# A matmul unit takes its last chunk at its very end, and background work of a decoder layer begins later

## The chip, the cores and the metric

The kernel runs on one core of a Trainium2 chip. The metric is the device time of one execution in microseconds; the median over several runs is compared. The engines of the core run their own instruction streams and meet at semaphores: TensorE (PE: matmuls), VectorE (DVE), ScalarE (ACT), GpSimd (POOL), and SyncE (SP), which issues the DMAs. The order of instructions on each engine is fixed when the program is built.

## The reference, cut to what matters

One layer of a decoder, in float32, for 512 prompt tokens and 64 sample tokens (576 in all) of width 1024:

```python
def swiglu(x, w_gate, w_up, w_down):
    return (jax.nn.silu(x @ w_gate) * (x @ w_up)) @ w_down

def decoder_layer(x, conv4_buf, lru_h0, conv31_buf, mem_k, mem_v, p):
    x = x + FFN_RES * rmsnorm(swiglu(rmsnorm(x, p['g_ff1_pre']), p['ff1_w_gate'], p['ff1_w_up'], p['ff1_w_down']), p['g_ff1_post'])
    mix, new_conv4, new_h, new_conv31 = token_mixer(rmsnorm(x, p['g_mix_pre']), conv4_buf, lru_h0, conv31_buf, p)
    x = x + rmsnorm(mix, p['g_mix_post'])
    x = x + rmsnorm(memory_attention(rmsnorm(x, p['g_mem_pre']), mem_k, mem_v, p['w_q'], p['w_o']), p['g_mem_post'])
    x = x + FFN_RES * rmsnorm(swiglu(rmsnorm(x, p['g_ff2_pre']), p['ff2_w_gate'], p['ff2_w_up'], p['ff2_w_down']), p['g_ff2_post'])
    return x, new_conv4, new_h, new_conv31
```

The hidden width of the two feed-forward blocks is 2816, which is 22 chunks of 128. The token mixer has a causal convolution over 31 positions, for which the sample tokens need 30 old rows of state each.

## The kernel before

**Products.** Every float32 operand is split in two parts, a first (h) and a second (l), and a matmul becomes three products: weight h by input h, weight h by input l ("highs"), and weight l by input h ("lows"). The 576 tokens are two halves of 288 columns. A *unit* is one output tile of 128 rows; for each half `mm` issues its products into one bank of PSUM: for 8 input chunks 16 highs and then 8 lows, 24 in all (21 for 7 chunks). `flow.until(... in xs.ready)` in `mm` lets the planner run until an input chunk has been planned; on the chip the product then waits for the semaphore of the engine that makes the chunk.

**Feed-forward.** `f1` and `f2` run in three groups of 8, 7 and 7 hidden chunks. In a group, each chunk has a gate unit and an up unit (`f1g`), and the result goes DVE, ACT, DVE, ACT, DVE: `f1s` (normalised gate product out of PSUM), silu on ACT, `f1u` (up product), `f1s<-f1s,f1u`, then `f1h_h` on ACT (first part) and `f1h_l` on DVE (second part). Behind the group come 8 down units (`f1d`) that take those chunks as their input, so the first down unit's last chunk is the one made last. The down sums are added up in `f1o` by DVE.

**Weights.** Each unit's weights come by DMA (`wraw`), ACT makes the first part (`wspl<-wraw`), POOL the second in four pieces of 256 columns (DVE at times). For 33 of the later units the second part is made ahead of time by `make_lows`: DMA in (`kraw`), a copy on ACT and a subtraction on DVE (both `khi`), and a DMA out to memory (`lows`), from which the unit loads it. Two such ways run side by side. They pause from two units before to the end of an edge between up and down units (`HOLD`).

**Old rows.** `old_rows` computes the part of the 31-tap convolution that depends on the old state only: for each of four pairs of chunks a DMA each (`st`, two buffers), one ACT instruction each, and 29 small DVE instructions each (`old<-st,par,old`), 232 on DVE and 8 on ACT in all. They don't pause at edges. The buffers of a pair are loaded again when DVE has read the pair before for the last time.

**What sets the order.** `Flow` is a planner that runs while the program is built. It keeps a made-up clock which the products push forward, and generators that yield until a time on that clock; the order in which they come up is the order of the instructions on every engine. `make_lows` starts at `KEPTAT` (its second way `KEPTGAP` later) and rests `KEPTGAP` after each piece, `old_rows` starts at `OLDROWS` and yields `OGAP` after each step. So what changes a planned time anywhere can move instructions later in the program too.

Of the kernel before, what the change touches and what calls it, by code (L numbers as in the profile page):

```python
# [65 lines left out]
X1 = 8  # L66
XSQ = 0.3
XSL = 2
OLDROWS = 80
OGAP = 1  # L70
KEPTAT = 25
KEPTGAP = 5
HOLD = 2
MEMORY = 150
MSL = 1
# [217 lines left out]
def trunk(ctx: ExitStack, tc: tile.TileContext, I, O):  # L293
# [6 lines left out]
    def dma(out, in_, eng=nc.sync):  # L300
        eng.dma_start(out=out, in_=in_)
        n = 1
        for _, c in out.ap:
            n *= c
        t = max(flow.now, flow.busy.get("d", 0.0)) + n * 4 / 300e3
        flow.busy["d"] = t
        flow.write(out, t + 2.0)

    def product(out, lhsT, rhs, start=True, stop=True):
        nc.tensor.matmul(out, lhsT, rhs, start=start, stop=stop)  # L310
        n = width(rhs)
        cost = 0.001 + max(n, 192) * 0.000457 if rhs.dtype == F32R else max(0.11, n * 0.00084)
        flow.product(cost, (lhsT, rhs), out)
# [16 lines left out]
    def bank(name):  # L330
        return psp.tile([P, 512], F32, tag="ps", name=name)
# [97 lines left out]
    def highs(ps, w, k, xs, half):  # L429

        hi, lo = xs.at(k, half)
        flow.settle(hi, lo)
        product(ps[:, :H], w[:, 0, k, :], hi, start=k == 0, stop=False)
        product(ps[:, :H], w[:, 0, k, :], lo, start=False, stop=False)

    def lows(ps, unit, xs, half):
        w, nk = unit
        for k in range(nk):
            product(ps[:, :H], w[:, 1, k, :], xs.at(k, half)[0], start=False, stop=k == nk - 1)
            flow.run()  # L440

    def mm(unit, xs, half, name):

        w, nk = unit
        ps = bank(name)
        for k in range(nk):
            flow.until(lambda: (k, half) in xs.ready)
            highs(ps, w, k, xs, half)
            flow.run()
        lows(ps, unit, xs, half)  # L450
        return ps

    def units_of(n, lead, xs, name, window=0):


        order = stream(n, lead, 0)
        if window:
            for at in range(0, n, window):
                us = [next_unit(j == 0) for j in range(window)]
                for half in range(2):  # L460
                    for j, u in enumerate(us):
                        if half and j:
                            ahead(state["used"] - window + j)
                        yield at + j, half, mm(u, xs, half, f"{name}_{at + j}_{half}")
            return
        for i, halves in order:
            u = next_unit()
            for half in halves:
                yield i, half, mm(u, xs, half, f"{name}_{i}_{half}")
# [102 lines left out]
    def fresh(name, n=KC):  # L572
        o = Operand(n)
        for c in range(n):
            o.hi[c], o.lo[c] = ring(f"{name}h{c}", F32R), ring(f"{name}l{c}", F32R)
        return o
# [227 lines left out]
    def project(o, xs, first, tail, name, lag=0, end=None):  # L804
# [38 lines left out]
        for m, halves in stream(n, 0, lag):  # L843
            u = next_unit()
            for half in halves:
                flow.spawn(evac(m, half, mm(u, xs, half, f"{name}_{m}_{half}")))
# [59 lines left out]
    def old_rows():  # L906

        for c0 in range(0, KC, 2):
            both = range(c0, c0 + 2)
            st = {}  # L910
            for c in both:
                st[c] = memp.tile([P, NB * GL], F32, tag="st", name=f"st{c}", bufs=2)
                dma(out=st[c], in_=I["conf_state"][c])
            yield wait(*st.values())
            for c in both:
                act.activation(out=tok(old[:, c, :]), in_=st[c].rearrange("p (b t) -> p b t", t=GL)[:, :, 0:NT],
                               func=AF.Identity, scale=cw[:, 0, c:c + 1], bias=V["conf_conv_b"][:, c:c + 1])
            for k in range(1, GS):
                yield OGAP
                n = min(NT, GS - k)  # L920
                for c in both:
                    o = tok(old[:, c, :])[:, :, :n]
                    vec.scalar_tensor_tensor(out=o, in0=st[c].rearrange("p (b t) -> p b t", t=GL)[:, :, k:k + n],
                                             scalar=cw[:, k, c:c + 1], in1=o, op0=ALU.mult, op1=ALU.add)

    def memory():
        raw = [memp.tile([P, 2 * NM], F32, tag=f"raw{q}", name=f"mraw{q}") for q in range(KC // 2)]
        for q in range(KC // 2):
            dma(out=raw[q].rearrange("p (c t) -> p c t", c=2),
                in_=I["mem"][2 * q:2 * q + 2].rearrange("c p t -> p c t"))  # L930
        x = [raw[c // 2][:, c % 2 * NM:(c % 2 + 1) * NM] for c in range(KC)]
        sqs = Squares(accs[2], KC, "mem")
        for c in range(KC):
            yield wait(x[c]) + 1
            sqs.add(x[c], NM)
        yield from sqs.whole()
        rbs = []
        yield from bcast_rsqrt(accs[2], "mem", rbs, 0, NM)
        yield wait(rbs[0])
        for c in range(KC):  # L940
            vec.scalar_tensor_tensor(out=x[c], in0=x[c], scalar=V["g_mem_kv"][:, c:c + 1], in1=rbs[0][:, :NM],
                                     op0=ALU.mult, op1=ALU.mult)
        for c in range(KC):
            t = ring(f"mT{c}", F32R)
            yield wait(x[c]) + 1
            split(t[:, 0:NM], t[:, NM:2 * NM], x[c], vec, lambda t=t: mT.append(t))

    def make_lows(way):

        for n, (src, nk, ncol) in enumerate(makes):  # L950
            if n % 2 != way:
                continue
            while any(e - HOLD <= state["used"] <= e for e in edges):
                yield 0.5
            cols = slice(0, nk * ncol)
            raw = memp.tile([P, 1024], F32, tag=f"kraw{way}", name=f"kraw{n}")
            hi = memp.tile([P, 1024], F32R, tag=f"khi{way}", name=f"khi{n}")
            dma(out=raw[:, cols].rearrange("p (k m) -> p k m", k=nk), in_=src)
            yield wait(raw)
            act.activation(out=hi[:, cols], in_=raw[:, cols], func=AF.Copy)  # L960
            yield wait(hi)
            vec.tensor_tensor(out=hi[:, cols], in0=raw[:, cols], in1=f32(hi[:, cols]), op=ALU.subtract)
            yield wait(hi) + 0.5
            dma(out=lows_[n, :, cols], in_=f32(hi[:, cols]))
            yield KEPTGAP

    for way in range(2):
        flow.spawn(make_lows(way), KEPTAT + way * KEPTGAP)
    flow.spawn(memory(), MEMORY)
    flow.spawn(old_rows(), OLDROWS)  # L970
    mixin = ffn("f1", F1LEAD, xg, ghalf[:, 0, :], V["g_mix_pre"], lambda: fresh("mn"), place=0, rbx=rbx)
# [13 lines left out]
    for m in range(KC):  # L985
        w, _ = next_unit()
        ps = bank(f"mk{m}")
# [318 lines left out]
    for m, half, ps in first4:  # L1306
        lows(ps, us[m], yl, half)
# [439 lines left out]
```

## Time and profile before

| | |
|---|---|
| median of 3 runs | 1474.09 us (1473.46 to 1474.64) |
| the profiled execution | 1476.8 us |
| its span in the trace | 1475.0 us |
| TensorE busy | 1422.6 us (96%) |
| VectorE busy | 879.8 us (60%) |
| GpSimd busy | 817.4 us (55%) |
| ScalarE busy | 723.5 us (49%) |
| mean granted clock of TensorE | 0.982 |

TensorE is busy for nearly the whole span, so the time is its work, its idle time, and what its clock adds when it is granted at half. The stages by time: `f1` to about 402 us and its last down units behind that, the mixer's input products (`z`), its output products (`wol`, `woc`), the queries, attention (about 910 to 1010), and `f2` to the end.

### The profile page before, as it was taken

The numbers are of one execution on the slowest core, as the hardware profiler recorded it, in microseconds if no ns is written. First come the engines' busy times: TensorE is split into PE (matmuls) and PEld (weight loads), VectorE is DVE, ScalarE is ACT, GpSimd is POOL, SyncE is SP. The second block draws the span as 40 slices with busy tenths as digits, with TensorE's granted clock in tenths as the row PEclk, the third lists the DMA queues.
The fourth block names the chain that finished last, engine by engine and source line by source line (L and its number), as shares of the span: only waits on it lengthen the run. The fifth ranks groups of instructions, "written<-read, shape, count | busy, mean of one in ns | idle before, by whom it ended". The sixth has DMA issues, their size and how long they took to land.

```text
span 1475.0 us, 27481 instructions
## 1 busy us (share of the span) xinstructions
PE 1422.6 (96%) x10550; PEld 1408.8 (96%) x10550; DVE 879.8 (60%) x1737; ACT 723.5 (49%) x1269; POOL 817.4 (55%) x1005
## 2 busy tenths in 40 slices
PE   8999999999999999999899999978999999999997
PEld 8999999999999999998699999878999999999997
DVE  7877887423356699999986776863633012312335
ACT  7544534322355568657847577764532222212233
POOL 7854445544356777676745566742464444444433
PEclk9999999999999999999999999998999999999998
DMA  6775766632388433223436787873642222222244
GB/s 234 224 264 182 250 216 228 211 89 85 116 291 306 131 106 93 92 92 123 160 117 223 259 297 268 278 274 126 232 151 86 75 84 85 76 88 85 80 137 140
DMA packets 89299, 245.34 MB, mean 166 GB/s; under 512 B 11984, under 2 KB 26576, under 8 KB 89168
## 3 DMA queue, kind: packets, MB, share of 16 engines
q1 hardware_dynamic: 84560, 235.66, 48.2%
q10 hardware_dynamic: 4608, 7.93, 1.5%
q8 instruction: 83, 1.36, 0.4%
q14 instruction: 48, 0.39, 0.1%
HBM read 215.76 MB, written 27.80 MB: 165 GB/s over the span
## 4 chain that ended last, share of the span: by engine, by line
PE 69%; DVE 19%; ACT 4%; POOL 3%; issue 3%; DMA 2%; SPq 0%; DVEq 0%; ACTq 0%; POOLq 0%
PE f2g L310 18%; PE f1g L310 13%; PE f2d L310 10%; PE f1d L310 9%; DVE cv L258 5%; PE z L310 3%; PE wol L310 3%; PE wo L310 3%; POOL wspl L258 2%; PE q L310 2%; PE woc L310 2%; DVE u L258 2%; PE mk L310 2%; DVE acc L258 1%; DVE cc L258 1%
## 5 line engine op out<-in xcount | busy, mean ns | idle before, releaser
L258 POOL TENSOR_TENSOR wspl<-wraw,wspl 128x256 fp32r<-128x256 f32 x840 | 654.1, 811 | 521.9 <-ACT wspl L258 518.0
L258 ACT ACTIVATE wspl<-wraw 128x1024 fp32r<-128x1024 f32 (+1 forms) x267 | 276.7, 1037 | 273.2 <-PE f2g L310 113.0
L310 PE MATMUL f1g<-xgh,wspl 128*128 128x288 f32 x1408 | 284.9, 297 | 0.0
L310 PE MATMUL f2g<-fnh,wspl 128*128 128x288 f32 x1408 | 281.3, 295 | 0.0
L310 PEld LDWEIGHTS f1g<-xgh,wspl 128*128 128x128 f32 x1408 | 228.2, 190 | 0.4 <-ACT xgh L258 0.2
L310 PEld LDWEIGHTS f2g<-fnh,wspl 128*128 128x128 f32 x1408 | 226.8, 188 | 0.0
L310 PE MATMUL z<-mnh,wspl 128*128 128x288 f32 x1024 | 206.0, 297 | 3.8 <-DVE gl L258 3.8
L310 PE MATMUL f1g<-xgl,wspl 128*128 128x288 f32 x704 | 192.0, 298 | 1.8 <-DVE xgl L258 1.8
L310 PE MATMUL f2g<-fnl,wspl 128*128 128x288 f32 x704 | 189.5, 295 | 0.0
L310 PEld LDWEIGHTS z<-mnh,wspl 128*128 128x128 f32 x1024 | 165.7, 190 | 4.2 <-issue 4.2
L310 PE MATMUL f1d<-f1h_h,wspl 128*128 128x288 f32 x704 | 143.9, 299 | 2.4 <-ACT f1h_h L258 2.4
L310 PE MATMUL f2d<-f2h_h,wspl 128*128 128x288 f32 x704 | 140.8, 295 | 0.0
L310 PE MATMUL z<-mnl,wspl 128*128 128x288 f32 x512 | 138.7, 297 | 0.0
L310 PEld LDWEIGHTS f1g<-xgl,wspl 128*128 128x128 f32 x704 | 133.7, 190 | 3.0 <-DVE xgl L258 2.7
L258 DVE SCALAR_TENSOR_TENSOR cv<-gl,par,cv 128x512 f32<-128x512 f32 x194 | 133.8, 745 | 0.0
L310 PEld LDWEIGHTS f2g<-fnl,wspl 128*128 128x128 f32 x704 | 132.5, 188 | 0.0
L310 PEld LDWEIGHTS f1d<-f1h_h,wspl 128*128 128x128 f32 x704 | 115.1, 191 | 2.6 <-ACT f1h_h L258 2.6
L310 PEld LDWEIGHTS f2d<-f2h_h,wspl 128*128 128x128 f32 x704 | 113.1, 188 | 0.0
L310 PE MATMUL f1d<-f1h_l,wspl 128*128 128x288 f32 x352 | 96.5, 299 | 0.7 <-DVE f1h_l L258 0.7
L258 DVE TENSOR_TENSOR f2u<-rbt,f2g 128x288 f32<-128x288 f32 x44 | 20.0, 454 | 129.1 <-PE f2g L310 129.1
L310 PEld LDWEIGHTS z<-mnl,wspl 128*128 128x128 f32 x512 | 96.8, 189 | 0.0
L310 PE MATMUL f2d<-f2h_l,wspl 128*128 128x288 f32 x352 | 94.8, 295 | 0.0
(324 smaller groups left out, 2661.2 us busy)
## 6 DMA issues: line engine op xcount, KB each, us to landing
wraw<-in_ff_w_gate SPq DMA_DIRECT2D x51, 512.0 KB, 3.7
wraw<-in_ff_w_up SPq DMA_DIRECT2D x50, 512.0 KB, 3.6
wspl<-lows SPq DMA_DIRECT2D x42, 512.0 KB, 4.2
wraw<-in_ff_w_down SPq DMA_DIRECT2D x46, 448.0 KB, 4.0
wraw<-in_w_in SPq DMA_DIRECT2D x32, 512.0 KB, 3.9
lows<-khi SPq DMA_DIRECT2D x26, 512.0 KB, 3.6
wraw<-in_w_out SPq DMA_DIRECT2D x24, 512.0 KB, 4.2
wraw<-in_ff_w_down SPq DMA_DIRECT2D x16, 512.0 KB, 3.6
```

Of the source, the lines that this page charges most:

```text
L258: return fn(*a, **k)
L310: nc.tensor.matmul(out, lhsT, rhs, start=start, stop=stop)
```

## The change

In `mm`, the last chunk's highs come behind the lows of all the other chunks, and its low last: for 8 chunks 14 highs, 7 lows, then 2 highs and 1 low. The last chunk is thus first used by product 22 rather than product 15 (for 7 chunks product 19 rather than 13). One other user of `highs` and `lows`, the first four units of `wol`, is as before. Three constants of the planner change: old rows start at 140 rather than 80, second parts made ahead at 130 rather than 25, and they rest 3 rather than 5.

```diff
-OLDROWS = 80
+OLDROWS = 140
 OGAP = 1
-KEPTAT = 25
-KEPTGAP = 5
+KEPTAT = 130
+KEPTGAP = 3
...
-    def lows(ps, unit, xs, half):
+    def lows(ps, unit, xs, half, ks=None):
         w, nk = unit
-        for k in range(nk):
+        for k in range(nk) if ks is None else ks:
             product(ps[:, :H], w[:, 1, k, :], xs.at(k, half)[0], start=False, stop=k == nk - 1)
             flow.run()
...
         for k in range(nk):
+            if k == nk - 1:
+
+                lows(ps, unit, xs, half, range(nk - 1))
             flow.until(lambda: (k, half) in xs.ready)
             highs(ps, w, k, xs, half)
             flow.run()
-        lows(ps, unit, xs, half)
+        lows(ps, unit, xs, half, (nk - 1,))
         return ps
```

The count of instructions on PE, ACT and POOL work is the same but for a few pieces that go to DVE instead of POOL. In the rows below a name carries the group, the chunk and the half (`f1s1_6_0`: group 1 of 0 to 2, chunk 6, half 0), and a running number of the tile.

DVE's instructions at the end of group 0, before, from the last chunk's first evacuation to its second part:

```order
L258 TENSOR_TENSOR f1s0_7_0_1536<-rbt_155,f1g0_14_0_1416 128x288
L258 TENSOR_TENSOR f1u0_7_0_1537<-rbt_155,f1g0_15_0_1497 128x288
L258 SCALAR_TENSOR_TENSOR old_161<-st0_1104,par_103,old_161 128x8x3
L258 SCALAR_TENSOR_TENSOR old_161<-st1_1106,par_103,old_161 128x8x3
L258 TENSOR_TENSOR f1s0_7_0_1536<-f1s0_7_0_1536,f1u0_7_0_1537 128x288
L258 SCALAR_TENSOR_TENSOR old_161<-st0_1104,par_103,old_161 128x8x2
L258 SCALAR_TENSOR_TENSOR old_161<-st1_1106,par_103,old_161 128x8x2
L258 SCALAR_TENSOR_TENSOR old_161<-st0_1104,par_103,old_161 128x8
L258 SCALAR_TENSOR_TENSOR old_161<-st1_1106,par_103,old_161 128x8
L258 TENSOR_TENSOR f1s0_7_1_1581<-rbt_155,f1g0_14_1_1461 128x288
L258 TENSOR_TENSOR f1u0_7_1_1582<-rbt_155,f1g0_15_1_1533 128x288
L258 TENSOR_TENSOR f1h0_l7_185<-f1s0_7_0_1536,f1h0_h7_184 128x288
```

The same place in the changed kernel:

```order
L258 TENSOR_TENSOR f1h0_l6_183<-f1s0_6_1_1316,f1h0_h6_182 128x288
L258 TENSOR_TENSOR f1s0_7_0_1412<-rbt_155,f1g0_14_0_1313 128x288
L258 TENSOR_TENSOR f1u0_7_0_1413<-rbt_155,f1g0_15_0_1379 128x288
L258 TENSOR_TENSOR f1s0_7_0_1412<-f1s0_7_0_1412,f1u0_7_0_1413 128x288
L258 TENSOR_TENSOR f1h0_l7_185<-f1s0_7_0_1412,f1h0_h7_184 128x288
```

No old row and no `khi` stands in group 0 any more; twelve old rows had also stood between `f1h0_l6` and `f1s0_7_0` before. The first `khi` now comes with the first down unit, and the first old rows a little behind it.

DVE at the end of group 1, before:

```order
L258 TENSOR_TENSOR f1h1_l5_2256<-f1s1_5_1_3235,f1h1_h5_2255 128x288
L258 TENSOR_TENSOR f1s1_6_0_3332<-rbt_155,f1g1_12_0_3232 128x288
L258 TENSOR_TENSOR f1u1_6_0_3333<-rbt_155,f1g1_13_0_3299 128x288
L258 TENSOR_TENSOR f1s1_6_0_3332<-f1s1_6_0_3332,f1u1_6_0_3333 128x288
L258 TENSOR_TENSOR f1h1_l6_2258<-f1s1_6_0_3332,f1h1_h6_2257 128x288
```

And in the changed kernel, where ten old rows of the fourth pair stand between `f1h1_l5` and the first row shown:

```order
L258 TENSOR_TENSOR f1s1_6_0_3218<-rbt_155,f1g1_12_0_3101 128x288
L258 TENSOR_TENSOR f1u1_6_0_3219<-rbt_155,f1g1_13_0_3179 128x288
L258 SCALAR_TENSOR_TENSOR old_161<-st6_3113,par_103,old_161 128x64
L258 SCALAR_TENSOR_TENSOR old_161<-st7_3115,par_103,old_161 128x64
L258 TENSOR_TENSOR f1s1_6_0_3218<-f1s1_6_0_3218,f1u1_6_0_3219 128x288
L258 SCALAR_TENSOR_TENSOR old_161<-st6_3113,par_103,old_161 128x64
L258 SCALAR_TENSOR_TENSOR old_161<-st7_3115,par_103,old_161 128x64
L258 SCALAR_TENSOR_TENSOR old_161<-st6_3113,par_103,old_161 128x64
L258 SCALAR_TENSOR_TENSOR old_161<-st7_3115,par_103,old_161 128x64
L258 TENSOR_TENSOR f1s1_6_1_3259<-rbt_155,f1g1_12_1_3145 128x288
L258 TENSOR_TENSOR f1u1_6_1_3260<-rbt_155,f1g1_13_1_3215 128x288
L258 TENSOR_TENSOR f1h1_l6_2069<-f1s1_6_0_3218,f1h1_h6_2068 128x288
```

Sixteen old rows have moved ahead of the second part on which the first down unit of group 1 waits. On ACT the fourth pair's start now stands right ahead of the same chunk's silu:

```order
L258 ACTIVATE f1s1_5_1_3104<-f1s1_5_1_3104 128x288
L258 ACTIVATE f1h1_h5_2066<-f1s1_5_1_3104 128x288
L258 ACTIVATE old_161<-st6_3113,par_103 128x64
L258 ACTIVATE old_161<-st7_3115,par_103 128x64
L258 ACTIVATE wspl46_3178<-wraw46_3002 128x896
L258 ACTIVATE f1s1_6_0_3218<-f1s1_6_0_3218 128x288
L258 ACTIVATE f1h1_h6_2068<-f1s1_6_0_3218 128x288
```

The two old instructions are new at this place; the rest of these rows stood there before in the same order. Some pieces of the mixer and of attention change places by a few instructions as well.

## Rows read from the trace of the kernel before

**Rows 1.** The page: part 1, and two lines of part 2 (40 slices).
```profile
PE 1422.6 (96%) x10550; PEld 1408.8 (96%) x10550; DVE 879.8 (60%) x1737; ACT 723.5 (49%) x1269; POOL 817.4 (55%) x1005
...
PEclk9999999999999999999999999998999999999998
```

**Rows 2.** Waits of TensorE by what released it: total, times, longest (us).
```profile
PE sot L310 <- ACT so L258: 6.9, 2, 6.4
PE wol L310 <- DVE yll L258: 4.1, 1, 4.1
...
PE f1d L310 <- ACT f1h_h L258: 2.4, 1, 2.4
...
PE spt L364 <- DVE ssum L258: 2.0, 2, 1.2
...
PE f1d L310 <- DVE f1h_l L258: 0.7, 1, 0.7
```

**Rows 3.** Timeline of TensorE at the first down unit: start, length, idle before.
```profile
120.65 0.29 PE L310 MATMUL f1d<-f1h_h,wspl 128*128 128x288 f32 x1
...
125.05 0.46 PE L310 MATMUL f1d<-f1h_h,wspl 128*128 128x288 f32 x1 [2.38 <-ACT f1h_h L258]
126.25 0.61 PE L310 MATMUL f1d<-f1h_l,wspl 128*128 128x288 f32 x1 [0.73 <-DVE f1h_l L258]
126.65 2.36 PE L310 MATMUL f1d<-f1h_h,wspl 128*128 128x288 f32 x9
```

**Rows 4.** Stretches: TensorE busy (products), granted clock, DMA share; last one `f2d` alone.
```profile
120.65:178.80 58.15, 55.04 (x396) 0.94 0.70 238
125.24:132.07 6.83, 6.10 (x25) 0.50 0.80 249
...
1142.37:1193.38 51.01, 51.01 (x384) 1.00 0.27 82
```

**Rows 5.** Timeline of VectorE at the first group's end.
```profile
114.98 1.75 DVE L258 TENSOR_TENSOR khi<-kraw,khi 128x1024 fp32r<-128x1024 f32 x1
116.66 2.84 DVE L258 SCALAR_TENSOR_TENSOR old<-st,par,old 128x64 f32<-128x64 f32 x4
119.43 1.01 DVE L258 TENSOR_TENSOR f1h_l<-f1s,f1h_h 128x288 fp32r<-128x288 f32 x1
120.37 2.75 DVE L258 SCALAR_TENSOR_TENSOR old<-st,par,old 128x64 f32<-128x64 f32 x12
123.04 0.44 DVE L258 TENSOR_TENSOR f1s<-rbt,f1g 128x288 f32<-128x288 f32 x1
...
125.75 0.44 DVE L258 TENSOR_TENSOR f1h_l<-f1s,f1h_h 128x288 fp32r<-128x288 f32 x1
```

**Rows 6.** Timeline of VectorE at the second group's end.
```profile
264.86 0.46 DVE L258 TENSOR_TENSOR f1u<-rbt,f1g 128x288 f32<-128x288 f32 x1 [1.19 <-PE f1g L310]
...
266.56 0.46 DVE L258 TENSOR_TENSOR f1h_l<-f1s,f1h_h 128x288 fp32r<-128x288 f32 x1 [0.51 <-ACT f1h_h L258]
```

**Rows 7.** Old rows: ns min/median/max; then one pair's start on ScalarE and VectorE.
```profile
L258 DVE SCALAR_TENSOR_TENSOR old<-st,par,old x232: 220/274/785, 93.4 to 240.8; 128x64 f32<-128x64 f32 x88, 128x56 f32<-128x56 f32 x4, 128x48 f32<-128x48 f32 x4, 128x40 f32<-128x40 f32 x4
...
205.71 0.44 ACT L258 ACTIVATE old<-st,par 128x64 f32<-128x64 f32 x1 [4.31 <-DMA st<-in_conf_state]
...
202.79 1.40 DVE L258 SCALAR_TENSOR_TENSOR old<-st,par,old 128x8 f32<-128x8 f32 x2
...
207.85 0.87 DVE L258 SCALAR_TENSOR_TENSOR old<-st,par,old 128x64 f32<-128x64 f32 x4
```

**Rows 8.** Two other waits of TensorE, and the clock of the stretches with them.
```profile
38.54 0.83 PE L310 MATMUL ssx<-ones,acc 128*128 128x1 f32 x6 [2.27 <-DVE acc L258]
...
703.18 0.40 PE L310 MATMUL lg<-xch,gwh 128*128 128x288 f32 x1 [2.34 <-DVE xc L258]
...
39.90:43.30 3.40, 3.40 (x16) 0.50 0.61 244
702.00:706.60 4.60, 3.42 (x16) 1.00 0.08 15
```

## The prediction, made before the changed kernel was run

> **What bounds the kernel now.** I read the page first, then TensorE's waits, then the stretches in which its clock is low, and only then the engine that made it wait. The page shows TensorE busy for 1422.6 of 1475.0 us [rows 1]; the reader sees that no other engine is near that, and that the granted clock is full in nearly every slice. So the work of TensorE is a floor that this change does not touch (the same products, in another order). What can move is its 52 us of idle time and the stretches at half clock that follow some waits. The list of waits [rows 2] has one entry that this change aims at: the first down unit of `f1` waits 2.38 us for `f1h_h` and 0.73 us for `f1h_l`. The others in that list lie in the mixer and in attention.
>
> The place itself: the first down unit starts at 120.65, has done its 14 highs of seven chunks, and stands until 125.05 and again until 126.25 [rows 3]. From 125.24 to 132.07 the clock granted is 0.50, which is the 1.2 GHz level, and 25 products take 6.10 us there [rows 4]. Elsewhere a product takes 51.01 / 384 = 0.133 us, from the down units of `f2`, which wait for nothing [rows 4]; 25 of them would be 3.32 us. So the half clock costs 2.78 us, the waits 3.11 us, and the place 5.9 us. As a check: `f1`'s eight units of this kind take 58.15 us and `f2`'s 51.01 [rows 4], 7.1 us more, of which the remaining 1.25 us belong to the 12 other products that stand among them.
>
> Why it waited: the up unit's half 0 of the last chunk ended 24 products before 120.65, at 117.46, but DVE took it out of PSUM only at 123.04 and gave the second part at 126.19, 8.7 us after the product. DVE had no gap since 114.98: one `khi` of 1.75 us, four old rows of 0.71 each, a second part of 1.01, twelve old rows of 0.23 each [rows 5]. Where DVE has neither old rows nor `khi` in front of it, at the end of group 1, the way from the released evacuation (264.86) to the second part (267.02) is 2.2 us [rows 6]. DVE, late with background work, bounds this place.
>
> **The change, part by part.**
>
> *Edge of group 0.* All old rows and all `khi` leave group 0. The last chunk then takes about 2.2 us, ready near 119.7, ahead of the down unit's start; its half 1, whose up unit ends at 120.65, is ready by about 123 and is needed only after 24 + 21 products, 6.0 us. Both waits go, and the half clock that came with them: -5.9 us. The new order of products alone would give 7 products, 0.93 us, of the 3.1.
>
> *Where the work goes.* The 33 second parts and 232 old rows still have to be done before the units that use them. DVE, ACT and the DMA queue have room in the down units of group 0, where DVE has no chunks to make. That part I cost at nothing: TensorE waits there for weights alone, none of which waits is in the list [rows 2]. If the cover were gone, the price would be a wait for `wspl`; before, the same DMA load beside the first down units (share 0.70 to 0.80, [rows 4]) caused none.
>
> *Edge of group 1.* Before, it cost nothing: the last chunk was made in 2.2 us [rows 6]. Now the fourth pair of old rows stands there: on DVE ten rows ahead of the last chunk's first evacuation, six more ahead of its second part; on ACT the pair's start right ahead of the chunk's silu. Queued behind them are `f1s`, `f1u`, `f1h_h` and `f1h_l` of that chunk, and for those the first down unit of group 1 waits. The time allowed, from the end of up half 0: its half 1, 24 products, then 18 products before the last chunk is used, and one more before its second part, 43 x 0.133 = 5.7 us. The old order would allow 0.8 us less.
>
> What the chunk takes now is not shown, so I bound it. From below 2.2 us, if DVE has caught up by then [rows 6]: no wait. From above 8.7 us, the last chunk of group 0 with sixteen old rows and a `khi` close in front [rows 5]: a wait of 3.0 us. In between: 2.2 us, plus sixteen old rows at 0.23, the price of the twelve in one run, 3.7 us, plus about half of a pair's start. A pair's start holds both engines: the old pair's last row ended at 204.19, the next pair's first began at 207.85, and ACT stood 4.31 us for the transfer [rows 7]. It takes 3.7 us, and I count 2 of them, since it begins ahead of the up unit's half. That is 7.9 us, a wait of 2.2 us. I take it rather than the upper bound since no `khi` of 1.75 us stands in that run.
>
> Whether the clock then falls is at its limit: a wait of 2.27 us at 38.54 was followed by a stretch at 0.50, one of 2.34 us at 703.18 by none [rows 8]. I take it that it does not fall at 2.2; if it falls, the price is that of the first edge, 2.8 us.
>
> Here a rule speaks against the change. The rows show one old row taking from 0.22 to 0.79 us, median 0.27 [rows 7], and the four slow ones at 116.66 stand beside the fast ones at 120.37 [rows 5]. The Trainium skill (GPSIMD Engine Reference, 1. Specifications) says that GpSimd shares its SBUF interfaces with VectorE and collides with its instructions that have two SBUF inputs; an old row has two, and the trace's two levels agree. By that rule the rows moved to group 1 run at the price that GpSimd's splits happen to leave them, which is the third rival below.
>
> *The rest.* In the mixer and in attention some pieces change places by a few instructions. The waits there are 6.9 us for `so`, 4.1 for `yll`, 2.0 for `ssum` [rows 2]. DVE's scores come a little earlier for some heads and later for others, so either sign is possible; I bound it at 4 us each way, less than the largest one of these waits, and take nothing.
>
> Sum: -5.9 + 2.2 = -3.7 us. The profiled execution was 1476.8 us with a span of 1475.0, 2.7 us above the median of 1474.1, so I take the difference from the median: 1470.4.
>
> **The rivals.** A change within 0.2%, 2.95 us, cannot be told from none.
>
> *The second edge pays it back.* The chunk takes 8.7 us as at the first edge, the wait is 3.0 us, the clock falls for 2.8: -5.9 + 5.8, 1474.0. For it: the sequence of DVE's rows is nearly the same. Against it: no `khi` stands in the run.
>
> *Slower: GpSimd on the old rows.* If its splits lie on the run, an old row takes 0.71 instead of 0.23, 0.48 more. With ten of sixteen, 4.8 us: the chunk takes 12.7, the wait is 7.0, with 2.8 for the clock 9.8: +3.9, 1478.0. It decides from eight rows on, a chunk of 11.8 us, where wait and clock pass 8.85. For it: GpSimd is busy 55% of the span [rows 1]. Against it: at the first edge only four of the sixteen rows were slow [rows 5].
>
> *Attention takes it.* A wait for `ssum` or `so` grows by some 3.5 us: 1473.9. The same places could as well give.
>
> *The change does not do what it says:* TensorE would still wait at the first edge, for a weight behind the transfers that now begin there. 1474 to 1477. Against it: those begin behind the edge.
>
> **How the numbers follow.** My forecast 0.45, the second edge 0.25, GpSimd 0.17, attention 0.09, no effect 0.04. The forecast's own range is 1468.2 (no wait at the second edge) to 1471.1. The whole range reaches to 1479, a microsecond above the third case with ten rows, and down to 1465.5, no wait at the second edge and 2.7 us given by attention. The three middle cases fall within 0.2% but for about 0.02 that are faster and 0.04 that are slower by what attention adds. Faster 0.47, same 0.32, slower 0.21.
>
> **What would show it.** Right: no wait of `f1d` for `f1h_h` near 120 and full clock there, `f1`'s first eight down units in 52 to 53 us; near 265 a wait of `f1d` of 1.5 to 2.5 us with the clock full behind it. The second edge paying back shows as a wait of 2.4 to 4 us there and a stretch at 0.50. GpSimd's rival shows old rows near 0.7 us between `f1h1_l5` and `f1h1_l6`. The forecast is wrong if the first down unit still waits, if the second edge costs more than 5 us or nothing, or if the sum of waits in attention moves by over 3 us.

## The result, and the profile after

The changed kernel takes 1483.19 us in the median of 6 runs (1480.42 to 1485.88), the kernel before 1473.78 us in 6 runs beside it (1471.55 to 1474.64): a ratio of 1.0064, 95% interval 1.005 to 1.0078. It is slower by 9.4 us, where 3.7 us less had been forecast. The profiled execution took 1484.2 us, with a span of 1482.4, against 1475.0 before. The two profiled executions differ by 7.4 us and not by 9.4, since that of the kernel before, 1476.8, was 3.0 us above the median of its six runs and that of the changed kernel 1.0; only the 7.4 can be placed.

The page, parts 1 and 2, beside [rows 1]:

```profile
PE 1429.3 (96%) x10550; PEld 1413.6 (95%) x10550; DVE 868.0 (59%) x1747; ACT 724.6 (49%) x1269; POOL 803.9 (54%) x998
...
PEclk9999999999999999999999999986999999999998
```

TensorE is busy for 6.7 us more with the same products, and idle for 0.7 us more (53.1 against 52.4). So the waits together are about as long as before, and more work runs at half clock (mean granted clock 0.977 against 0.982). Some of that lies in attention (the digits 8 and 6 of the clock), where waits shrank in exchange, so the loss is read stage by stage, waits and clock together. TensorE's waits by releaser (total, times, longest), beside [rows 2]:

```profile
PE ssx L310 <- DVE acc L258: 5.0, 2, 3.8
PE f1d L310 <- ACT f1h_h L258: 3.4, 1, 3.4
...
PE sot L310 <- ACT so L258: 1.9, 2, 1.5
PE ssmem L310 <- DVE acc L258: 1.7, 1, 1.7
...
PE f1d L310 <- DVE f1h_l L258: 0.8, 1, 0.8
```

`f1d` still waits for `f1h_h` and `f1h_l`, longer than before; the wait for `so` has shrunk from 6.9 to 1.9 us, and that of `ssmem` is new. Which edge the wait of `f1d` belongs to, the timeline of TensorE tells:

```profile
266.22 0.29 PE L310 MATMUL f1d<-f1h_h,wspl 128*128 128x288 f32 x1
...
272.22 0.61 PE L310 MATMUL f1d<-f1h_h,wspl 128*128 128x288 f32 x1 [3.45 <-ACT f1h_h L258]
273.62 0.61 PE L310 MATMUL f1d<-f1h_l,wspl 128*128 128x288 f32 x1 [0.80 <-DVE f1h_l L258]
```

It is no longer the edge of group 0 (120 us) but that of group 1: the first down unit there starts at 266.22 and stands 3.45 us for the last chunk's first part and 0.80 us for its second. In numbers, the down units of group 0 and a stretch at low clock in them, then the same for group 1 (length, TensorE busy, products, granted clock, DMA share and GB/s):

```profile
121.57:176.26 54.69, 53.01 (x390) 0.97 0.68 226
171.90:178.70 6.80, 6.79 (x41) 0.75 0.73 234
266.22:318.10 51.88, 47.63 (x338) 0.93 0.68 238
272.20:279.00 6.80, 5.98 (x23) 0.51 0.71 260
```

Group 1's down units take 51.88 us; before, the same products took 44.64 with no wait. Nearly all of the 7.24 us are the two waits, 4.25, and 23 products that took 5.98 us at a clock of 0.51, where 3.05 is their time at full clock. Group 0's take 54.69 us against 58.15 in [rows 4] (57.98 counted from the first of them to the next gate unit): its edge is free, but not all of the 5.9 us of gain arrived.

The whole difference of the two profiled executions, from stretches cut at the same products (first of a stage to first of the next): lead and group 0 +0.9 us, its down units -3.3, group 1 +0.7, its down units +7.2, group 2 and its down units +0.5, memory keys to output projection +1.9, `f2` to the end -0.5. That is 7.4, as in the spans.

### The profile page after: what moved, and what is told of

It reads as the page before. It is cut to its first block, busy times and chain, and to the rows that moved or that the text cites. A ratio compares the mean times of both kernels' runs of the same rounds, so it can differ in the third digit from the quotient of the medians.

```text
span 1482.4 us, 27472 instructions
## 1 busy us (share of the span) xinstructions
PE 1429.3 (96%) x10550; PEld 1413.6 (95%) x10550; DVE 868.0 (59%) x1747; ACT 724.6 (49%) x1269; POOL 803.9 (54%) x998
```

## The experiments

Eleven kernels were run; each ratio is against the kernel before, run on the same chip in the same session.

**The order alone** (the three constants as before):

```diff
-OLDROWS = 140
-KEPTAT = 130
-KEPTGAP = 3
+OLDROWS = 80
+KEPTAT = 25
+KEPTGAP = 5
```

> Only the new order of products in every unit; old rows and second parts begin as before. Theory A (the loss lies at the edge of group 1, where old rows now stand): that edge is free again, the wait at the edge of group 0 shrinks from 3.1 to about 2.2 us, with or without the half clock behind it, so 1470 to 1474 us. Theory B (the loss comes from what the new order does in the mixer and in attention): 1476 to 1480 us.

1475.65 us against 1474.33, ratio 1.0002 (0.9987 to 1.0016). The first down unit of group 0, and its eight units:

```profile
125.03 0.40 PE L310 MATMUL f1d<-f1h_h,wspl 128*128 128x288 f32 x1 [1.81 <-ACT f1h_h L258]
126.23 0.40 PE L310 MATMUL f1d<-f1h_l,wspl 128*128 128x288 f32 x1 [0.80 <-DVE f1h_l L258]
...
120.26:175.19 54.93, 52.31 (x395) 1.00 0.74 252
```

The wait went from 3.11 to 2.61 us and the clock stayed full, so the eight units take 54.93 instead of 57.98. Group 1's edge is free (44.53). So the order by itself gives about 3 us at this place in this one execution; in the median the two kernels could not be told apart. The edge of group 1 came free, as theory A said, and the wait at group 0 shrank by 0.5 us where it had named about 0.9; the time lies 1.7 us above its band, just below that of B.

**The constants alone** (old order of products, `OLDROWS` 140, `KEPTAT` 130, `KEPTGAP` 3):

> Only the three constants; the units' products in the old order. Theory A: the first down unit of group 1 waits about 0.8 us longer than the 4.25 us of the changed kernel, its eight down units take 52 to 53 us against 44.6 before, and the time is 1480 to 1485 us. Theory B: 1468 to 1474 us, since the edge of group 0 is free and the later stages are as before.

1480.26 us against 1474.33, ratio 1.0039 (1.0026 to 1.0053). The first down unit of group 1, then its eight units:

```profile
270.07 0.40 PE L310 MATMUL f1d<-f1h_h,wspl 128*128 128x288 f32 x1 [3.48 <-ACT f1h_h L258]
271.48 0.61 PE L310 MATMUL f1d<-f1h_l,wspl 128*128 128x288 f32 x1 [1.01 <-DVE f1h_l L258]
...
264.84:317.07 52.23, 47.74 (x339) 0.93 0.64 228
```

The wait is 4.49 us with the half clock behind it: the loss at this edge comes with the constants, whatever the order of products. Theory A holds, but for the size of what the order gives here: the wait grew by 0.24 us, not by 0.8. The main run of the fourth pair's rows also begins 0.8 us earlier here, against the down unit (table below).

**Old rows that pause at edges**, in the changed kernel:

```diff
             for k in range(1, GS):
                 yield OGAP
+                while any(e - HOLD <= state["used"] <= e for e in edges):
+                    yield 0.5
```

> The changed kernel, with old rows that pause from two units ahead of an edge to its end, as the second parts made ahead do. Theory A: no wait of the first down unit of group 1 or one under 1 us, its eight units in 45 to 46 us, 6 to 7 us less than the changed kernel: 1475 to 1478 us. Theory B: 1482 to 1484 us, as the changed kernel.

1475.1 us against 1474.33, ratio 1.0011 (0.9998 to 1.0025); the profiled execution was one of the longest of its 12, 1480.29. Down units of group 1:

```profile
266.40:310.93 44.53, 44.53 (x338) 1.00 0.72 256
```

The edge of group 1 is free: 160 old rows instead of 190 stand ahead of the second part that its first down unit waits for. With only old rows held back, 0.5% of the 0.6% have gone: those thirty were the main cause of the loss. The time is in the band of theory A. But with both edges free the kernel is no faster than before the change; what is missing is taken up below.

**The new order in the first feed-forward block only**, constants as changed:

```diff
-            if k == nk - 1:
+            if k == nk - 1 and name.startswith("f1"):
...
-        lows(ps, unit, xs, half, (nk - 1,))
+        lows(ps, unit, xs, half, (nk - 1,) if name.startswith("f1") else None)
```

> The changed kernel, with the new order of products only in the units of the first feed-forward block; all later units in the old order. Theory A: as the changed kernel but for what the later stages lost, about 2 us, 1480 to 1482 us. Theory B: the loss is gone, 1472 to 1476 us.

1482.46 us against 1474.33, ratio 1.005 (1.0032 to 1.0068). Group 1's down units, then the stages from the memory keys to the output projection:

```profile
266.16:317.68 51.52, 47.81 (x338) 0.93 0.65 236
455.64:1043.79 588.15, 554.02 (x4072) 0.97 0.54 182
```

The same stages in the changed kernel:

```profile
455.97:1044.84 588.87, 560.39 (x4073) 0.96 0.54 181
```

588.15 us with the old order in these stages, 588.87 with the new: the new order has less idle time there (28.5 against 34.1 us) and as much more at half clock. Theory B is refuted; the time is 0.5 us above the band of A. So most of the loss does not lie in the mixer and attention. A cost of about 2 us there is not excluded: over all profiled kernels these stages took 586.3 to 590.4 us with the new order everywhere (mean of eight 588.7) and 584.9 to 588.3 with the old order in them (mean of five 586.9).

**Four buffers for the old state** (`bufs=2` to `bufs=4` for `st`), in the changed kernel:

> The changed kernel with four buffers instead of two for the old state, so that the fourth pair's transfer does not wait for VectorE's last old row of the third; the instructions stand in the same order but for the pair's start a few places earlier. Theory A1 (the pair's start, ScalarE and VectorE standing for the transfer, makes the edge of group 1 late): the wait there falls from 4.25 to about 2.5 us, with or without the half clock, and the time to 1477 to 1481 us. Theory A2 (the old rows themselves, slowed by GpSimd's splits, make it late): the wait stays between 3.5 and 4.5 us and the time between 1481 and 1484 us.

1477.08 us against 1475.72, ratio 1.0019 (1.0008 to 1.0031). VectorE's ten old rows ahead of the last chunk of group 1, and the down units:

```profile
262.47 3.95 DVE L258 SCALAR_TENSOR_TENSOR old<-st,par,old 128x64 f32<-128x64 f32 x10
...
266.34:313.20 46.86, 45.19 (x338) 1.00 0.72 254
```

The fourth pair's rows begin at once behind chunk 5, 3.9 us ahead of the down unit, not 0.3 us as in the changed kernel. Two waits of 0.83 and 0.84 us are left, the clock stays full, and 5.0 of the 7.2 us are back. So standing for transfers was the larger part, as A1 said, and the gain is larger than it said. But the edit frees every pair of its stand, not the fourth alone: in the changed kernel ScalarE also stood 3.51 and 1.72 us for the third pair's transfers, here not at all, and the third pair ends 5.1 us ahead of the down unit instead of 2.8. So 2.3 of the 3.6 us of lead were there before the fourth pair began. The remaining 1.67 us of wait stand behind the old rows that are still at the edge; no run took them away with four buffers.

**Only the old rows late** (`KEPTAT` 25 and `KEPTGAP` 5, `OLDROWS` 140):

> The changed kernel, with the second parts made ahead beginning at 25 and resting 5 as before; only the old rows begin late (at 140). The twelve subtractions of group 1 are then eleven, the old rows at its edge 26 instead of 28. Theory A: the edge of group 0 is free, that of group 1 waits about 4 us with the half clock behind it, 1479 to 1484 us. Rival (second parts that begin late crowd group 1): the wait at the edge of group 1 falls below 2 us and the time to 1473 to 1476 us.

1475.2 us against 1475.72, ratio 1.0006 (0.9994 to 1.0017). The start of the fourth pair on VectorE, and group 1's down units:

```profile
258.00 0.28 DVE L258 SCALAR_TENSOR_TENSOR old<-st,par,old 128x64 f32<-128x64 f32 x1 [2.17 <-ACT old L258]
258.50 1.07 DVE L258 SCALAR_TENSOR_TENSOR old<-st,par,old 128x64 f32<-128x64 f32 x5 [0.22 <-ACT old L258]
...
261.99:307.59 45.60, 44.79 (x338) 1.00 0.50 173
```

Theory A expected 4 us of wait here and it was 0.81, in half 1, with 26 old rows still at the edge. Its simple form, that old rows at an edge cost, is refuted; the rival's numbers came. What differs at the edge is that the pair begins 4.0 us ahead of the down unit instead of 0.3. The last 37 us ahead of the down unit hold four subtractions in either kernel, and the lead is older than that. The second row of the third pair stands 35.2 us ahead of the down unit in the changed kernel and 39.1 us ahead here, as the second in a run of four (changed kernel first):

```profile
231.07 0.28 DVE L258 SCALAR_TENSOR_TENSOR old<-st,par,old 128x64 f32<-128x64 f32 x1 [1.72 <-ACT old L258]
...
222.67 0.87 DVE L258 SCALAR_TENSOR_TENSOR old<-st,par,old 128x64 f32<-128x64 f32 x4
```

And the second pair, from its first row to its last, takes 35.3 us there and 29.8 here (length, VectorE busy on its 58 rows, clock, DMA):

```profile
191.52:226.84 35.32, 21.90 (x58) 1.00 0.61 214
...
188.50:218.28 29.78, 19.53 (x58) 1.00 0.61 227
```

In the changed kernel five subtractions stand among these rows, here four; the rows themselves take 2.4 us longer there, with 19 of the 58 over 0.4 us instead of 15. So with the late rhythm of the second parts VectorE is late two pairs ahead of the edge already. That is the rival's crowding, and it comes early in group 1.

**Only the second parts late** (`OLDROWS` 80, `KEPTAT` 130, `KEPTGAP` 3):

> The changed kernel, with the old rows beginning at 80 as before; only the second parts begin late (130, rest 3). Theory A: no old row is left at the edge of group 1, so that edge is free; at the edge of group 0, 24 old rows but no subtraction: a wait of 0.5 to 2.5 us without the half clock. 1471 to 1476 us. Rival (late second parts cost): 1478 to 1483 us.

1476.43 us against 1475.72, ratio 1.0004 (0.9991 to 1.0016). No wait of `f1d` is left at either edge; at group 0, where theory A expected 0.5 to 2.5 us, 24 old rows without a subtraction among them cost nothing. The time is 0.4 us above its band. Late second parts alone do not slow the kernel by what a measurement can tell. But the kernel gains nothing either, with both edges free; a wait of 3.8 us for `ssx` early on takes some of it.

**The new order and the pause**, constants as before:

> The new order of products and old rows that pause at edges, all three constants as before the change. Theory A: neither edge waits, both groups of down units take 51 to 53 and 44.6 us, 5 to 6 us less than before the change: 1467 to 1470 us. Rival (what the edges give is lost again later, as in the kernel with the order alone): 1472 to 1476 us.

1471.72 us against 1475.72, ratio 0.9977 (0.9966 to 0.9988). Down units of groups 0 and 1:

```profile
120.32:172.12 51.80, 51.80 (x394) 1.00 0.70 247
261.53:306.06 44.53, 44.53 (x338) 1.00 0.51 176
```

Neither edge waits; the first group's units take 51.80 us instead of 57.98. The edges came as theory A said; the time lies between the two bands, 0.3 us below the rival's.

**The pause alone**, in the kernel before:

> The kernel before the change, whose old rows pause at edges; order of products and constants as before. Theory A (what an edge costs is set by the background work in front of it, and 0.8 to 0.9 us of allowance only shifts it): both edges are free without the new order, the first eight down units take 51 to 53 us, 1467 to 1471 us. Rival (the new order is needed): the first down unit of group 0 still waits 1 to 3 us, 1471 to 1475 us.

1470.48 us against 1475.88, ratio 0.9963 (0.9951 to 0.9975). Down units of groups 0 and 1, and VectorE's way from the last chunk's up product of group 0 to its second part:

```profile
120.58:172.41 51.83, 51.83 (x394) 1.00 0.68 246
261.64:306.96 45.32, 44.89 (x338) 1.00 0.58 198
```

```profile
117.59 0.45 DVE L258 TENSOR_TENSOR f1u<-rbt,f1g 128x288 f32<-128x288 f32 x1 [3.38 <-PE f1g L310]
...
119.33 0.46 DVE L258 TENSOR_TENSOR f1h_l<-f1s,f1h_h 128x288 fp32r<-128x288 f32 x1 [0.51 <-ACT f1h_h L258]
```

The up unit releases VectorE at 117.59 and the second part is there at 119.79, 2.2 us later: VectorE had caught up. Group 1 keeps one wait of 0.43 us. The time is in the band of theory A. The gain that the change aimed at is had with the two added lines of the pause; neither the new order nor the constants are needed.

**The order in the first block, and the pause** (constants as before):

> The kernel with the new order and the pause, all constants as before, with the new order only in the first feed-forward block. Theory (the later stages are worth the same in either order, what one gives the other takes): within 2 us of the kernel with the order everywhere and the pause, 1469 to 1473 us. Rival (the new order costs in attention): 1466 to 1469 us.

1472.10 us against 1475.88, ratio 0.9972 (0.9961 to 0.9983), in the band of the theory. It cannot be told apart from the kernel with the order everywhere (0.9977), nor from the pause alone (0.9963).

**A rest of five** (`KEPTGAP` back to 5 in the changed kernel):

> The changed kernel with the second parts resting 5 instead of 3 between pieces; they still begin at 130. In group 1 eleven subtractions instead of twelve stand on VectorE, but the last two right ahead of the fourth pair of old rows, and 21 instead of 28 old rows at the edge. If the backlog in front of the pair decides, the wait at the edge of group 1 stays at 3 to 5 us with the half clock, 1480 to 1484 us; if the number of old rows at the edge decides, it falls below 2 us and the time to 1475 to 1478 us.

1477.93 us against 1475.88, ratio 1.0018 (1.0008 to 1.0028). The fourth pair's first rows, and TensorE's waits in group 1's down units:

```profile
263.33 2.73 DVE L258 SCALAR_TENSOR_TENSOR old<-st,par,old 128x64 f32<-128x64 f32 x8
...
268.67 0.40 PE L310 MATMUL f1d<-f1h_h,wspl 128*128 128x288 f32 x1 [0.73 <-ACT f1h_h L258]
269.68 0.40 PE L310 MATMUL f1d<-f1h_l,wspl 128*128 128x288 f32 x1 [0.62 <-DVE f1h_l L258]
...
273.70 0.40 PE L310 MATMUL f1d<-f1h_l,wspl 128*128 128x288 f32 x1 [0.96 <-DVE f1h_l L258]
```

The time is in the second band, the wait of 2.3 us in three pieces just above what it said, without half clock. The pair begins 2.1 us ahead of the down unit's start at 265.39, and with fewer old rows at the edge than the kernel with only the old rows late (21 against 26) this one waits longer: their number does not decide.

Put together: how long before the first down unit of group 1 the main run of the fourth pair's rows begins on VectorE, what that unit then waits in half 0, and the clock behind it. Each row is one profiled execution.

| kernel | begins ahead by, us | waits, us | clock behind |
|---|---|---|---|
| changed | 0.3 (one row), then from -0.5 | 3.45 + 0.80 | half |
| constants alone | 2.7 (one row), then 0.3 | 3.48 + 1.01 | half |
| order in first block | 0.7 | 2.71 + 1.00 | half |
| rest of five | 2.1 | 0.73 + 0.62 | full |
| four buffers | 3.9 | 0.83 | full |
| only old rows late | 4.0 (one row), then 3.5 | none (0.81 in half 1) | full |

## Why the prediction was wrong

**The edge of group 0** was right in its mechanism: of the eleven kernels only the one with the order alone, which keeps both old rows and `khi` ahead of it, waits there, and the pause alone shows the price, 57.98 to 51.83 us, 6.2 against the 5.9 predicted.

**The step that failed is the edge of group 1**, sized at a wait of 2.2 us, 3.0 at most, with a full clock. It was 4.25 us with 2.9 us of half clock, 7.2 in all, past the 5 us that the prediction itself had named as a sign of being wrong. The rival "the second edge pays it back" named the place and the mechanism and put its price at 5.8. The allowance of 5.7 us was right (the first down unit had done its 18 products 5.7 us after the up half's end). The chunk took 10.5 us, not 7.9: its up half ended 24 products ahead of 266.22, at 263.03, and its second part was there at 273.57. VectorE in that stretch of the changed kernel:

```profile
253.23 1.22 DVE L258 TENSOR_TENSOR khi<-kraw,khi 128x1024 fp32r<-128x1024 f32 x1
254.36 2.95 DVE L258 SCALAR_TENSOR_TENSOR old<-st,par,old 128x64 f32<-128x64 f32 x6
257.24 1.21 DVE L258 TENSOR_TENSOR khi<-kraw,khi 128x1024 fp32r<-128x1024 f32 x1
...
262.19 1.24 DVE L258 SCALAR_TENSOR_TENSOR old<-st,par,old 128x8 f32<-128x8 f32 x2
...
265.91 0.28 DVE L258 SCALAR_TENSOR_TENSOR old<-st,par,old 128x64 f32<-128x64 f32 x1 [1.14 <-ACT old L258]
266.67 3.53 DVE L258 SCALAR_TENSOR_TENSOR old<-st,par,old 128x64 f32<-128x64 f32 x9 [0.48 <-ACT old L258]
270.12 0.44 DVE L258 TENSOR_TENSOR f1s<-rbt,f1g 128x288 f32<-128x288 f32 x1
...
273.12 0.45 DVE L258 TENSOR_TENSOR f1h_l<-f1s,f1h_h 128x288 fp32r<-128x288 f32 x1
```

The upper bound of 8.7 us had been taken from a run of old rows that was already under way. Here the third pair ends only at 263.43, the next pair's rows start at 265.91, and the ten ahead of the chunk reach to 270.12: the first evacuation comes 7.1 us after the up product, the second part 3.45 us behind that. In the terms of the prediction's sum, the pair's start took 3.6 us (263.03 to 266.67) where 2 were counted, the ten rows 3.45 where 2.3 were, and the rest, six rows and the chunk's own way, 3.45 where 3.6 were. I had counted 2 us of a pair's start since "it begins ahead of the up unit's half"; it began behind it. Nor was the missing `khi` a ground for the lower value: two stood at 253.23 and 257.24, among the old rows that made VectorE late for this pair. The transfer that ScalarE stood for:

```profile
265.43 0.44 ACT L258 ACTIVATE old<-st,par 128x64 f32<-128x64 f32 x1 [1.15 <-DMA st<-in_conf_state]
```

The stand of 1.15 us is only its end, ScalarE having had other work; four buffers, which take away this stand and those of the third pair, took 2.6 of the 4.25 us of wait and the half clock with them. How far VectorE lags when a pair ends was the quantity on which all hung. I took it from one place in the trace of before, and an order tells which instruction comes first, not when.

**"Where the work goes", costed at nothing,** failed too, for 2.6 of the 5.9 us. The cover named was TensorE waiting for weights alone in group 0's down units. But a small product for the memory's statistics, `ssmem`, stands there and takes VectorE's `acc`, between whose steps old rows lie. TensorE and VectorE around it:

```profile
171.91 0.61 PE L310 MATMUL ssmem<-ones,acc 128*128 128x1 f32 x4 [1.68 <-DVE acc L258]
...
169.30 0.97 DVE L258 TENSOR_TENSOR acc<-acc,sqmem 128x256 f32<-128x256 f32 x1
170.19 1.33 DVE L258 SCALAR_TENSOR_TENSOR old<-st,par,old 128x64 f32<-128x64 f32 x4
171.44 0.41 DVE L258 TENSOR_TENSOR acc<-acc,sqmem 128x256 f32<-128x256 f32 x1
```

A wait of 1.68 us, and behind it the stretch with a clock of 0.75 (171.90 to 178.70, above). The old rows alone do not explain it: eleven stood between the steps of `acc` before the change, without a wait, and 13 stand there in the kernel with only the old rows late, which has none either and takes 51.8 us for these units; here it is 13 too. The wait goes with the rhythm of the second parts. In the five kernels that have both the late old rows and second parts at 130 with a rest of 3, changed kernel included, it is 1.68 to 1.70 us; with a rest of five or with old rows at 80 it is 0.7; with second parts at 25 there is none. How one leads to the other was not followed further.

**The mixer and attention**, bounded at 4 us each way and taken at nothing, came to +1.9 in this pair of executions; with the order taken back in these stages 588.2 us were measured against 588.9, so the bound held. Whether the order costs a little there is not settled (see that experiment). Inside, `so` gave 5.0 us back, and other waits and half clock took more.

**GpSimd on the old rows** was a part and not the cause by itself. Its splits lay on the last of the nine rows that took 3.53 us:

```profile
267.56 2.56 POOL L258 TENSOR_TENSOR wspl<-wraw,wspl 128x256 fp32r<-128x256 f32 x4 [2.46 <-ACT wspl L258]
```

Row by row, the five that began before 267.60 took 0.28 to 0.29 us, three within the splits 0.76 to 0.77, and the last, which outlasted them, 0.49. Together, each overlapping the next a little, they took 3.53 us, where nine at the prediction's 0.23 are 2.1. That accounts for the 1.15 us by which the ten rows were sized too low; it is far from the rival's ten slow rows and 4.8 us. With four buffers ten such rows took 3.95 us, and the wait still fell to 1.67.

**Not foreseen:** `ssx` waits 5.0 us in the lead instead of 2.3, 1.19 us at a first place that had no wait before and 3.79 at the one of [rows 8], where TensorE now comes 0.7 us earlier (35.59) and VectorE 0.8 us later (39.33). In the stages before the first down unit that is +0.9 us.

**The second edge is not the whole miss.** For a free second edge the forecast had 1468.2 of 1474.1 us, a ratio of 0.996. Three kernels with the new order have group 0's edge free and group 1's free or nearly so, and came to 1.0011 (the pause in the changed kernel), 1.0006 (only old rows late) and 1.0004 (only second parts late): 6 to 7 us of the forecast gain are missing outside the two edges. The 5.9 us may also be too much for a median, having been read from one execution that was 2.7 us above it; the pause alone kept its whole gain, though (0.9963). The profiles place only part of it: against the kernel before, the stages ahead of the first down unit and those from memory keys to output projection took 2.5 and 3.5 us more with the pause in the changed kernel, 0.5 and 3.4 more with only the second parts late, and 0.4 and 0.7 less with only the old rows late.

What stays open: where the rest of those 6 to 7 us goes, and how the rhythm of the second parts makes the second pair of old rows 5.5 us longer; the extra subtraction and the rows that fell beside GpSimd's splits were not tried apart. Each kernel was profiled once, and the 12 runs of the order alone, for one, have granted clocks from 0.976 to 0.985, so a stage's difference under about 2 us is no proof by itself.

## What to carry to other kernels

Background work that is pushed back from one dependency edge can arrive at the next one; move it only together with a rule that keeps it away from every edge, and that rule may be all that is needed (0.9963 by itself). Price such an edge from VectorE's lag at the place where the work will stand, the time it stands for transfers included, and not from a run of the same work that was seen elsewhere. Where the clock falls behind a wait of TensorE, count the half clock too: at group 1 it cost 2.9 us on top of 4.25 us of wait, and with four buffers 2.6 us of wait went and 2.4 us of busy time with them.

## What the runs showed of the hardware

The length of a wait alone did not tell whether the clock falls. The wait for `ssmem` was 1.68 us in the changed kernel, with a granted clock of 0.75 over the 6.8 us behind it, and 1.69 us with the constants alone, where the clock stayed full:

```profile
172.23 0.61 PE L310 MATMUL ssmem<-ones,acc 128*128 128x1 f32 x4 [1.69 <-DVE acc L258]
...
170.00:178.00 8.00, 6.31 (x49) 1.00 0.74 248
```

The same wait of 1.7 us was followed by half clock in the kernels with the order in the first block and with four buffers too, and by full clock with the pause in the changed kernel.

At the edge of group 0 waits of 1.81 and 0.80 us (the order alone) left it full, where 2.38 and 0.73 us [rows 3] had it at half. What an old row costs beside GpSimd shows in single rows of 128x64: 0.76 to 0.77 us within its splits at 267.66 to 269.79 and 0.28 outside, at 266.87 to 267.54, in the changed kernel. And 12 runs of one kernel spread over 5 to 9 us, which I had not expected from the 1.2 us spread of the three runs of before.
